# GpSimd's state products in pieces of 256 or 384 columns, retention's decay in VectorE's addition

## The chip, the cores and the metric

The kernel runs on one core of a Trainium2 chip. The metric is the time of the program on the device in microseconds (us). The core has the engines TensorE (PE in the profile; its weight loads are PEld), VectorE (DVE), ScalarE (ACT), GpSimd (POOL) and SyncE (SP, which issues the DMAs). They run side by side and wait for one another by semaphores; each runs its own instructions in the order in which the program gives them.

## The reference

One inference step of a hybrid decoder trunk with two layers, on 16 meta tokens and 256 prompt tokens of one sequence, and on 8 sample sequences of 4 new tokens each: T = 304 columns in all. A layer is

```
proj  = rmsnorm(x) @ w_in
mixed = concat(gated delta net, RG-LRU, GLA, retention) * silu(gate)
x     = x + mixed @ w_out
```

Three of the four mixers carry matrix states. For each sequence and head, after the new tokens,

```
delta      S' = S * exp(g_last)     + sum_j k_j (decay_j v_new_j)^T     128 x 128, 4 heads
GLA        S' = diag(exp(b_last)) S + sum_j k_j (decay_j v_j)^T          64 x 128, 4 heads
retention  S' = S * gamma_h^n       + sum_j k_j (decay_j v_j)^T          64 x 128, 4 heads
```

where n is the number of tokens in the chunk, and b_last and gamma_h are GLA's and retention's decays. Outputs are the normalised x of prompt and samples and all new states, of the prompt and of the eight samples.

## The kernel before

The activations stand transposed, 128 features on the partitions and the 304 tokens in the columns. Each float32 matrix is split into two parts, hi and lo, of TensorE's faster float32 type, and each product takes three matmuls (xh by hi, xl by hi, xh by lo). The weights stream through in units of 128 x 512: a DMA brings `raw`, ScalarE copies it to `hi`, VectorE subtracts to get `lo`. A layer has 48 tiles of the input projection (4 units each) and 16 of the output projection. These products (tiles `main`) are most of TensorE's work.

The mixers run in the gaps of that stream. They are written as Python generators: after a few of the stream's matmuls the builder asks each generator whether its next step may be emitted, by a small model of the engines' clocks (class `Clocks`, prices in `price`, one for each engine and size). The model's prices so set the order in which all engines get their work; on the chip the order is then fixed. One generator runs the four delta heads (two at a time; PSUM tiles named `d`), one GLA's two pairs of heads, one the RG-LRU and retention's two pairs (PSUM tiles `e`).

The states of a head or a pair are one tile `S9` of 128 x 9 x 128: the prompt's state and the eight samples' (tiles `s9.0` to `s9.4` in the rows). Late in `delta_thread` and `pair_thread` each tile goes through the same steps: `reads` multiplies the queries with the old states on TensorE; GpSimd multiplies S9 by the decay; `advance` makes the update on TensorE in PSUM and VectorE adds it to S9. For the samples the update needs the values laid out by sequence: `spread` multiplies the values, repeated n times, by a mask of blocks, into `vm`. Delta calls it once for eight samples, GLA and retention twice for four each.

Three more operations come up below. `lq` is VectorE's subtraction that gives the low part of a squared output for the norm's sum (`totals`: `hq` by ScalarE, `lq` by VectorE, then two matmuls with `onesr`); `zq` is GLA's scaled query for one level of its within-chunk scores, read by a matmul with `zk`; the conv taps are multiply-adds `acc<-ct,par,acc` of the short convolutions. `spots`, four copies on GpSimd for each of two sources, gathers columns into `lxd`, which `reads` takes.

Of the kernel before, what the change touches and what calls it, by code (L numbers as in the profile page):

```python
# [9 lines left out]
F32 = mybir.dt.float32  # L10
# [343 lines left out]
def trunk(ctx: ExitStack, tc: tile.TileContext, I, O):  # L354
    nc = tc.nc
    clk = Clocks()
    pe, act, dve, pool, sp = (Engine(e, k, clk) for e, k in ((nc.tensor, "P"), (nc.scalar, "A"), (nc.vector, "V"),
                                                             (nc.gpsimd, "G"), (nc.sync, "S")))
    mul, add, sub = ALU.mult, ALU.add, ALU.subtract
# [51 lines left out]
    def C(name, a=0, n=1):  # L411
        return cst[:, CC[name] + a:CC[name] + a + n]
# [22 lines left out]
    els = one.tile([128, 12], F32, name="els")  # L435
# [408 lines left out]

    def spread(vm, R, blocks):

        n = blocks.shape[1]
        pool.tensor_mul(vm, R[:, None, 128:256].bitcast(F32).to_broadcast([128, n, 128]),
                        blocks[:, :, None].to_broadcast([128, n, 128]))

    def copies(out, x, n):

# [2 lines left out]
            pool.tensor_copy(out=out[:, 128 * b:128 * b + 16 * n].rearrange("p (u t) -> p u t", u=n),  # L855
                             in_=x[:, None, c:c + 16].to_broadcast([128, n, 16]))

    def advance(tag, S9, p0, n, products):
        ps = pt(tag)
        for i, (out, k, v) in enumerate(products):  # L860
            pe.matmul(ps[out, :128 * n], k, v, start=i == 0 or out.start > 0,
                      stop=i + 1 == len(products) or products[i + 1][0].start > 0)
        dve.tensor_add(S9[:, p0:p0 + n, :], S9[:, p0:p0 + n, :],
                       ps[:, :128 * n].rearrange("p (b v) -> p b v", v=128))

    busy = []

# [31 lines left out]
    def delta_thread(l, p, tag):  # L899
# [4 lines left out]
        K, Q, V, KN, VB, KTL, Eb, AT, qe, egl = ({} for _ in range(10))  # L904
# [16 lines left out]
        for h in range(2):  # L921
            ps = yield from totals(tag, s[h][:, :T])
# [15 lines left out]
        for h in range(2):  # L938
            for src, d, k in ((V, VB, 1), (KN, KTL, 3)):
                d[h] = yield from take(1, src is V)  # L940
                ps = pt(tag)
# [49 lines left out]
        for r in range(2):  # L991
            for u in range(2):
                n = 512 - 16 * u
# [4 lines left out]
        for j in range(15):  # L998
            n, m = 15 - j, j // 2 + 1
# [39 lines left out]
        for h, c, a in hca:  # L1039
            r = slice(32 * a, 32 * a + 32)  # L1040
# [6 lines left out]
        for h, c, a in hca:  # L1047
            r = slice(32 * a, 32 * a + 32)
# [53 lines left out]
        VN, SS, S9 = {}, {}, {}  # L1102
# [7 lines left out]
        ps = pt(tag)  # L1110
# [5 lines left out]
        ps = pt(tag)  # L1116
# [5 lines left out]
        ps = pt(tag)  # L1122
        for h in range(2):
            pe.matmul(ch(ps, h), KN[h][:, 128:256], SS[h][:, 0:128], start=True, stop=True)
        for h in range(2):
            dve.scalar_tensor_tensor(ch(VB[h], 1), ch(ps, h), col[:, 2, 1, hs[h]:hs[h] + 1], ch(VB[h], 1),
                                     op0=mul, op1=add)
        yield
        ps = pt(tag)
# [5 lines left out]
        ps = pt(tag)  # L1135
# [5 lines left out]
        LQ, SL, R = {}, {}, {}  # L1141
# [5 lines left out]
        ps = pt(tag)  # L1147
# [4 lines left out]
        for h in range(2):  # L1152
            R[h], LQ[h] = yield from take(2)
            R[h] = recast(R[h], F32R)
            pk = pt(tag)
            pe.transpose(pk[:, 0:128], KN[h][:, 256:384], ident)
            pool.memset(LQ[h][:, 0:128], 0.0)
            sc = col[:, 3, 2, hs[h]:hs[h] + 1]
            hi_lo(R[h][:, 0:128], pk[:, 0:128], 64, sc)
            activ(LQ[h][0:16, 0:128], pk[0:16, 0:128], AF.Copy, scale=sc[0:16])  # L1160
            spots(lx["d"], 0, slice(0, 128), KN[h])
            spots(lx["d"], 1, slice(0, 128), qe[h])
            give(KN[h])
            yield
            pr = reads(tag, lx["d"], S9[h])
            activ(SL[h][:, 0:128], pr, AF.Copy)
            pool.tensor_mul(S9[h], S9[h], egl[h][:, 2:11, None].to_broadcast([128, 9, 128]))
            yield
        for h in range(2):
            ps = pt(tag)  # L1170
# [6 lines left out]
        for h in range(2):  # L1177
# [4 lines left out]
            ps = pt(tag)  # L1182
# [14 lines left out]
        for h in range(2):  # L1197
            vm = recast((yield from take9()), F32R)
# [84 lines left out]
    def pair_thread(l, p, m, tag):  # L1283
# [23 lines left out]
        S9 = yield from take9()  # L1307
# [44 lines left out]
        if m == "r":  # L1352
            yield from bg.vacant(tag, 2)
            ps2 = [pt(tag), pt(tag)]
            for c, (c0, n) in enumerate(CH):
                for h in range(2):
                    r = slice(64 * h, 64 * h + 64)
# [5 lines left out]
        for h in range(2):  # L1363
            ps = pt(tag)
# [82 lines left out]
        R = yield from take(2)  # L1447
        R = [recast(x, F32R) for x in R]
        ps, ps2 = pt(tag), pt(tag)
# [9 lines left out]
        else:  # L1459
            for h in range(2):  # L1460
                for c in range(2):
                    b = 128 * c + 64 * h
# [4 lines left out]
        for b in range(2):  # L1467
            hm = C("hs", 0, 2)[:, :, None].to_broadcast([128, 2, 64])
            v, k = ps2[:, 128 * b:128 * b + 128], ps2[:, 256 + 128 * b:384 + 128 * b]
# [5 lines left out]
            for h in range(2):  # L1475
                r, own = slice(64 * h + 32, 64 * h + 64), slice(64 * h, 64 * h + 64)
                if sc is None:
                    dve.tensor_sub(R[b][r, own], k[r, own], R[b][r, own].bitcast(F32))
                else:
                    dve.scalar_tensor_tensor(R[b][r, own], k[r, own], sc[r], R[b][r, own].bitcast(F32),  # L1480
                                             op0=mul, op1=sub)
            activ(R[b][:, 128:256], v, AF.Copy)
            dve.scalar_tensor_tensor(R[b][:, 128:256], R[b][:, 128:256].bitcast(F32), C("um", 0), v,
                                     op0=mul, op1=add)
# [7 lines left out]
        ps = pt(tag)  # L1492
        for c in range(2):
            for h in range(2):
                b = 128 * c + 64 * h
# [10 lines left out]
        pr = reads(tag, lx[m], S9)  # L1506
        activ(sel[:, 0:128], pr, AF.Copy)
        if m == "g":
            pool.tensor_mul(S9, S9, els[:, 2:11, None].to_broadcast([128, 9, 128]))
        else:  # L1510
            pool.tensor_scalar(S9[:, 0, :], S9[:, 0, :], C("dec", 3 * p + 1), None, op0=mul)
            pool.tensor_scalar(S9[:, 1:9, :], S9[:, 1:9, :], C("dec", 3 * p + 2), None, op0=mul)
        yield
        sqs_ = yield from take(2)
        yield from bg.vacant(tag, 2)
        ps = [pt(tag), pt(tag)]
        for h in range(2):
            r = slice(64 * h, 64 * h + 64)
# [9 lines left out]
        for h in range(2):  # L1528
# [3 lines left out]
            give(sqs_[h])  # L1532
        give(sel, SS, qe)
        advance(tag, S9, 0, 1, [(slice(64 * h, 64 * h + 64), ktb[:, 64 * h:64 * h + 64], VT[h][0:16, 256:384])
                                for h in range(2)])
        give(*VT)
        vm = recast((yield from take9()), F32R)
        for b in range(2):
            spread(vm[:, 4 * b:4 * b + 4], R[b], C("m4", 0, 4))
        yield  # L1540
        for b in range(2):
            advance(tag, S9, 1 + 4 * b, 4, [(slice(0, 128), R[b][:, 0:128], vm[:, 4 * b:4 * b + 4, :])])
            yield
        give9(recast(vm, F32))
        give(*[recast(x, F32) for x in R])
# [168 lines left out]
    for u, (l, ph, e, q) in enumerate(units):  # L1714
# [30 lines left out]
        a, b = ([t[:, k, :] for k in range(KT)] for t in (xh, xl)) if ph == "in" else (mh, ml)  # L1745
# [21 lines left out]
        if q == NH - 1:  # L1767
# [4 lines left out]
            kind, i = ORDER[e]  # L1772
# [109 lines left out]
```

## Time and profile before

| what | value |
|---|---|
| median of three runs | 1091.02 us (1091.01 to 1096.0) |
| profiled execution, time on the device | 1089.9 us |
| its span, first to last instruction | 1088.0 us |
| TensorE / its weight loads busy | 96% / 91% of the span |
| VectorE / ScalarE / GpSimd busy | 69% / 59% / 38% of the span |
| granted TensorE clock, mean | 0.991 |

The engines' shares are means over the whole span. TensorE is busy nearly throughout, so the waits that count are TensorE's; an idle stretch of another engine costs nothing by itself. Matmuls overlap in the records (one of 304 columns is shown with some 0.30 us and the next starts 0.14 us later), so a wait in the timeline is counted from the end of the last record to the next start.

### The profile page before, as it was taken

What the parts mean: (1) busy time and instruction counts of PE and PEld (TensorE: products, weight loads), DVE (VectorE), ACT (ScalarE), POOL (GpSimd) and SP (SyncE); (2) the same over time, 40 slices, a digit from 0 to 9 for tenths busy, and PEclk for the clock granted to TensorE, in tenths of its full rate; (3) what the DMA queues carried; (4) which work ended last, traced back from release to release, by engine and by line L of the source; (5) the groups of instructions that cost most, each with busy time, mean ns of one, the idle gap of its engine ahead of it and who ended that gap; (6) DMA issues with size and microseconds to landing.
All of it is one profiled execution on the core that took longest, in us unless ns stands there. A gap on an engine that the chain in (4) does not pass through costs nothing.

```text
span 1088.0 us, 23535 instructions
## 1 busy us (share of the span) xinstructions
PE 1042.6 (96%) x8358; PEld 995.1 (91%) x8358; DVE 746.0 (69%) x1457; ACT 639.7 (59%) x1438; POOL 412.9 (38%) x843
## 2 busy tenths in 40 slices
PE   8999999998999999999999998999999999899995
PEld 7899988988998999999999998888999998899995
DVE  5867588798656467556667757878886576765664
ACT  6677954665745766455455876555765466554542
POOL 4423374534518343022222348344254346211110
PEclk9999999999999999999999999999999999999998
DMA  6555434545465555666644545336545663566563
GB/s 212 188 150 187 134 123 138 189 148 190 139 208 186 174 165 181 198 208 211 206 134 144 178 149 164 126 102 212 178 152 159 201 214 122 176 202 207 184 191 138
DMA packets 116893, 186.86 MB, mean 172 GB/s; under 512 B 22184, under 2 KB 45368, under 8 KB 116776
## 3 DMA queue, kind: packets, MB, share of 16 engines
q1 hardware_dynamic: 116776, 185.37, 53.1%
q8 instruction: 65, 1.06, 0.4%
q14 instruction: 52, 0.43, 0.1%
HBM read 164.10 MB, written 19.96 MB: 169 GB/s over the span
## 4 chain that ended last, share of the span: by engine, by line
PE 67%; DVE 13%; DMA 5%; POOL 5%; issue 5%; ACT 4%; SPq 1%; DVEq 0%; ACTq 0%; POOLq 0%
PE main L302 55%; PE e L302 6%; PE d L302 5%; DMA raw<-in_w_in_dram 4%; DVE lo L302 4%; DVE m L302 2%; DVE n L302 2%; POOL m L302 2%; ACT hi L302 1%; DVE zq L302 1%; DVE acc L302 1%; POOL s9.4_4198 L302 1%; POOL n L302 1%; ACT L369 1%; SPq L302 1%
## 5 line engine op out<-in xcount | busy, mean ns | idle before, releaser
L302 PE MATMUL main<-xh,hi 128*128 128x304 f32 (+2 forms) x1488 | 468.7, 315 | 2.8 <-ACT xh L302 2.5
L302 DVE TENSOR_TENSOR lo<-raw,hi 128x512 fp32r<-128x512 f32 (+1 forms) x513 | 391.7, 782 | 101.6 <-ACT hi L302 100.0
L302 PE MATMUL main<-xh,lo 128*128 128x304 f32 (+2 forms) x1488 | 449.8, 302 | 4.2 <-DVE lo L302 4.2
L302 ACT ACTIVATE hi<-raw 128x512 fp32r<-128x512 f32 (+1 forms) x513 | 316.7, 625 | 228.6 <-PE main L302 95.9
L302 PE MATMUL main<-xl,hi 128*128 128x304 f32 (+2 forms) x1488 | 447.6, 301 | 0.4 <-DVE xl L302 0.3
L302 PEld LDWEIGHTS main<-xh,hi 128*128 128x128 f32 x1488 | 281.8, 189 | 14.8 <-issue 6.8
L302 PEld LDWEIGHTS main<-xh,lo 128*128 128x128 f32 x1488 | 281.6, 189 | 7.3 <-DVE lo L302 7.1
L302 PEld LDWEIGHTS main<-xl,hi 128*128 128x128 f32 x1488 | 282.2, 190 | 2.7 <-DVE xl L302 0.9
L302 PE MATMUL main<-m,hi 128*128 128x304 f32 (+1 forms) x1024 | 208.7, 298 | 0.0
L302 PEld LDWEIGHTS main<-m,hi 128*128 128x128 f32 x1024 | 166.5, 188 | 0.0
L302 PE MATMUL main<-m,lo 128*128 128x304 f32 (+1 forms) x512 | 153.3, 299 | 0.0
L302 POOL TENSOR_TENSOR ssq<-ssq,n 128x304 f32<-128x304 f32 (+1 forms) x29 | 34.8, 1200 | 167.4 <-ACT n L302 167.4
L302 PEld LDWEIGHTS main<-m,lo 128*128 128x128 f32 x512 | 96.1, 188 | 0.0
L302 POOL COPY cvo<-ct 128x3 f32<-128x3 f32 x64 | 31.6, 522 | 136.1 <-DVE ct L302 136.0
L302 POOL TENSOR_TENSOR n<-n,n 128x304 f32<-128x304 f32 (+1 forms) x38 | 35.5, 951 | 113.7 <-ACT n L302 69.1
L302 ACT ACTIVATE n<-n 128x304 f32<-128x304 f32 (+4 forms) x118 | 49.5, 438 | 36.0 <-DVE n L302 26.0
L302 DVE TENSOR_TENSOR n<-main,n 128x304 f32<-128x304 f32 (+1 forms) x32 | 14.9, 466 | 61.3 <-PE main L302 51.8
L369 ACT ACT_TABLE_LOAD x35 | 44.9, 1283 | 0.6
L302 DVE SCALAR_TENSOR_TENSOR acc<-ct,par,acc 128x328 f32<-128x328 f32 x64 | 40.7, 636 | 4.9 <-ACT acc L302 3.8
L302 ACT ACTIVATE m<-m 128x304 f32<-128x304 f32 (+5 forms) x95 | 39.3, 431 | 6.9 <-DVE m L302 3.1
L302 DVE TENSOR_TENSOR n<-main,rstd 128x304 f32<-128x304 f32 (+1 forms) x42 | 19.5, 465 | 26.4 <-PE main L302 26.0
L302 ACT ACTIVATE n<-e 128x304 f32<-128x304 f32 (+5 forms) x67 | 19.6, 307 | 28.9 <-PE e L302 15.4
(416 smaller groups left out, 1334.5 us busy)
## 6 DMA issues: line engine op xcount, KB each, us to landing
raw<-in_w_in_dram SPq DMA_DIRECT2D x383, 256.0 KB
raw<-in_w_out_dram SPq DMA_DIRECT2D x128, 256.0 KB
n<-o_dram SPq DMA_DIRECT2D x28, 152.0 KB
o_dram<-m SPq DMA_DIRECT2D x19, 152.0 KB
m<-in_x_dram SPq DMA_DIRECT2D x16, 152.0 KB
n<-in_x_dram SPq DMA_DIRECT2D x16, 152.0 KB
xs_dram<-n SPq DMA_DIRECT2D x16, 152.0 KB
n<-xs_dram SPq DMA_DIRECT2D x16, 152.0 KB
```

Of the source, the lines that this page charges most:

```text
L302: r = f(*a, **k)
L369: nc.scalar.preload_act_table_set(want[0])
```

## The change

GpSimd's decay of a state tile, one product of 9 x 128 = 1152 columns, becomes three products of 3 x 128 = 384 (function `decay`), for delta and GLA. `spread` makes one product for each two samples, 256 columns, where it made one of 1024 (delta) or 512 (GLA, retention). Retention's decay, two single-input scalings on GpSimd, is left out; `advance` gets the decay as an argument and VectorE's addition becomes a multiply-add, S9 * decay + update. The values computed are the same.

```diff
@@ -844,9 +844,14 @@
 
     def spread(vm, R, blocks):
 
-        n = blocks.shape[1]
-        pool.tensor_mul(vm, R[:, None, 128:256].bitcast(F32).to_broadcast([128, n, 128]),
-                        blocks[:, :, None].to_broadcast([128, n, 128]))
+        for i in range(0, blocks.shape[1], 2):
+            pool.tensor_mul(vm[:, i:i + 2], R[:, None, 128:256].bitcast(F32).to_broadcast([128, 2, 128]),
+                            blocks[:, i:i + 2, None].to_broadcast([128, 2, 128]))
+
+    def decay(S9, by):
+
+        for i in range(0, 9, 3):
+            pool.tensor_mul(S9[:, i:i + 3], S9[:, i:i + 3], by[:, i:i + 3, None].to_broadcast([128, 3, 128]))
 
     def copies(out, x, n):
 
@@ -855,13 +860,16 @@
             pool.tensor_copy(out=out[:, 128 * b:128 * b + 16 * n].rearrange("p (u t) -> p u t", u=n),
                              in_=x[:, None, c:c + 16].to_broadcast([128, n, 16]))
 
-    def advance(tag, S9, p0, n, products):
+    def advance(tag, S9, p0, n, products, by=None):
         ps = pt(tag)
         for i, (out, k, v) in enumerate(products):
             pe.matmul(ps[out, :128 * n], k, v, start=i == 0 or out.start > 0,
                       stop=i + 1 == len(products) or products[i + 1][0].start > 0)
-        dve.tensor_add(S9[:, p0:p0 + n, :], S9[:, p0:p0 + n, :],
-                       ps[:, :128 * n].rearrange("p (b v) -> p b v", v=128))
+        o, x = S9[:, p0:p0 + n, :], ps[:, :128 * n].rearrange("p (b v) -> p b v", v=128)
+        if by is None:
+            dve.tensor_add(o, o, x)
+        else:
+            dve.scalar_tensor_tensor(o, o, by, x, op0=mul, op1=add)
 
     busy = []
 
@@ -1164,7 +1172,7 @@
             yield
             pr = reads(tag, lx["d"], S9[h])
             activ(SL[h][:, 0:128], pr, AF.Copy)
-            pool.tensor_mul(S9[h], S9[h], egl[h][:, 2:11, None].to_broadcast([128, 9, 128]))
+            decay(S9[h], egl[h][:, 2:11])
             yield
         for h in range(2):
             ps = pt(tag)
@@ -1506,10 +1514,7 @@
         pr = reads(tag, lx[m], S9)
         activ(sel[:, 0:128], pr, AF.Copy)
         if m == "g":
-            pool.tensor_mul(S9, S9, els[:, 2:11, None].to_broadcast([128, 9, 128]))
-        else:
-            pool.tensor_scalar(S9[:, 0, :], S9[:, 0, :], C("dec", 3 * p + 1), None, op0=mul)
-            pool.tensor_scalar(S9[:, 1:9, :], S9[:, 1:9, :], C("dec", 3 * p + 2), None, op0=mul)
+            decay(S9, els[:, 2:11])
         yield
         sqs_ = yield from take(2)
         yield from bg.vacant(tag, 2)
@@ -1532,14 +1537,15 @@
             give(sqs_[h])
         give(sel, SS, qe)
         advance(tag, S9, 0, 1, [(slice(64 * h, 64 * h + 64), ktb[:, 64 * h:64 * h + 64], VT[h][0:16, 256:384])
-                                for h in range(2)])
+                                for h in range(2)], C("dec", 3 * p + 1) if m == "r" else None)
         give(*VT)
         vm = recast((yield from take9()), F32R)
         for b in range(2):
             spread(vm[:, 4 * b:4 * b + 4], R[b], C("m4", 0, 4))
         yield
         for b in range(2):
-            advance(tag, S9, 1 + 4 * b, 4, [(slice(0, 128), R[b][:, 0:128], vm[:, 4 * b:4 * b + 4, :])])
+            advance(tag, S9, 1 + 4 * b, 4, [(slice(0, 128), R[b][:, 0:128], vm[:, 4 * b:4 * b + 4, :])],
+                    C("dec", 3 * p + 2) if m == "r" else None)
             yield
         give9(recast(vm, F32))
         give(*[recast(x, F32) for x in R])
```

The planner prices the new instructions and the order of all engines moves with them from the first cut product on. Three places:

VectorE, layer 1, second delta pair, the second head's norm (its `lq` is the last one of a delta head), rows of before:

```order
L302 TENSOR_TENSOR lo<-raw,hi 128x512 x2
L302 TENSOR_TENSOR m_12588<-n_154,m_12587 128x288
L302 TENSOR_TENSOR m_12590<-n_5487,m_12589 128x288
L302 TENSOR_TENSOR lo<-raw,hi 128x512
L302 TENSOR_TENSOR lq<-g_144,hq 128x304
L302 TENSOR_TENSOR n_4200<-main,rstd 128x288
L302 TENSOR_TENSOR lo<-raw,hi 128x512
```

and of the change:

```order
L302 TENSOR_TENSOR s9.1_10369<-s9.1_10369,d 128x128
L302 TENSOR_TENSOR lo<-raw,hi 128x512 x2
L302 TENSOR_TENSOR lq<-n_167,hq 128x304
L302 TENSOR_TENSOR n_12715<-main,rstd 128x288
L302 TENSOR_TENSOR lo<-raw,hi 128x512 x2
L302 SCALAR_TENSOR_TENSOR g_147<-g_147,par,n_167 128x304
```

Ahead of this head's `lq` stood two subtractions of the gated output (`m`) and a `lo`; now `lo` twice alone.

GpSimd, layer 1, second delta pair, from the first head's decay (`egl`) on to the second head's gathering copies (`lxd`); rows of before:

```order
L302 TENSOR_TENSOR s9.1_11583<-s9.1_11583,egl 128x1152
L302 MEMSET g_144 128x128
L302 COPY lxd<-g_138 128x16
L302 COPY lxd<-g_138 128x3x4 x2
L302 COPY lxd<-g_138 128x2x4
L302 COPY lxd<-m_7452 128x16
L302 COPY lxd<-m_7452 128x3x4 x2
L302 COPY lxd<-m_7452 128x2x4
L302 TENSOR_TENSOR s9.0_4398<-s9.0_4398,egl 128x1152
```

and of the change:

```order
L302 TENSOR_TENSOR s9.0_11594<-s9.0_11594,egl 128x384 x3
L302 TENSOR_TENSOR s9.3_12530<-n_12204,cst 128x256 x2
L302 TENSOR_TENSOR s9.3_12530<-n_12205,cst 128x256 x2
L302 TENSOR_TENSOR n_157<-n_157,n_5929 128x288
L302 TENSOR_TENSOR g_140<-g_140,n_5378 128x288
L302 MEMSET n_167 128x128
L302 COPY lxd<-g_146 128x16
L302 COPY lxd<-g_146 128x3x4 x2
```

The second head's copies stood right behind the first head's decay; now the pieces of a retention pair's spread (`s9.3`), two gating products and a memset stand between.

GpSimd, layer 1, the spread of the last GLA pair and what is next to it; rows of before:

```order
L302 TENSOR_TENSOR g_146<-g_146,n_5970 128x304
L302 MEMSET g_146 128x16
L302 TENSOR_SCALAR s9.0_4398<-s9.0_4398,cst 128x128
L302 TENSOR_SCALAR s9.0_4398<-s9.0_4398,cst 128x1024
L302 TENSOR_TENSOR s9.2_11289<-n_10787,cst 128x512
L302 TENSOR_TENSOR s9.2_11289<-m_10788,cst 128x512
L302 TENSOR_TENSOR s9.3_171<-s9.3_171 80x15 x2
```

and of the change:

```order
L302 TENSOR_TENSOR g_134<-g_134,m_7481 128x304
L302 MEMSET g_134 128x16
L302 TENSOR_TENSOR s9.2_11411<-m_10886,cst 128x256 x2
L302 TENSOR_TENSOR s9.2_11411<-m_10887,cst 128x256 x2
L302 TENSOR_TENSOR s9.0_11535<-n_11148,cst 128x256 x2
L302 TENSOR_TENSOR s9.0_11535<-n_11149,cst 128x256 x2
L302 TENSOR_TENSOR s9.3_171<-s9.3_171 80x15 x2
```

Retention's two scalings are gone, and the spread of the first retention pair (`s9.0_11535`), which stood 14 rows further on, follows that of the last GLA pair: eight pieces in a row.

## Rows read from the trace of the kernel before

**Rows 1.** The page: busy time of each engine, share of the span, instructions.
```profile
PE 1042.6 (96%) x8358; PEld 995.1 (91%) x8358; DVE 746.0 (69%) x1457; ACT 639.7 (59%) x1438; POOL 412.9 (38%) x843
```

**Rows 2.** Windows view, three stretches: length, busy time (instructions), clock, DMA.
```profile
183.00:420.00 237.00, 229.05 (x1955) 215.25 (x1949) 164.03 (x332) 145.40 (x353) 112.60 (x229) 1.00 0.52 169
420.00:667.00 247.00, 246.04 (x1787) 240.98 (x1786) 159.22 (x284) 146.43 (x299) 71.92 (x133) 1.00 0.57 182
667.00:960.00 293.00, 278.71 (x2445) 262.23 (x2446) 214.75 (x446) 168.96 (x411) 132.30 (x273) 0.99 0.52 167
```

**Rows 3.** Timeline of TensorE: start, duration, instruction, [wait <- what ended it].
```profile
247.08 0.42 PE L302 MATMUL e<-zq,zk 128*64 128x64 f32 x7 [2.74 <-DVE zq L302]
...
419.58 0.41 PE L302 MATMUL d<-lq,onesr 128*128 128x304 f32 x1 [1.44 <-DVE lq L302]
...
733.25 0.41 PE L302 MATMUL e<-lq,onesr 128*128 128x304 f32 x1 [1.71 <-DVE lq L302]
...
746.61 0.50 PE L302 MATMUL d<-s9.1_10128,m 128*128 128x512 f32 x1 [2.18 <-DVE s9.2_3655 L302]
...
909.59 0.66 PE L302 MATMUL d<-s9.0_4398,lxd 128*32 128x128 f32 x11 [0.80 <-POOL lxd L302]
...
922.76 0.41 PE L302 MATMUL e<-lq,onesr 128*128 128x304 f32 x1 [0.54 <-DVE lq L302]
...
939.32 0.62 PE L302 MATMUL d<-lq,onesr 128*128 128x304 f32 x1 [3.03 <-DVE lq L302]
```

**Rows 4.** Timeline of GpSimd: three long products.
```profile
416.84 2.35 POOL L302 TENSOR_TENSOR s9.4_5925<-n,cst 128x1024 fp32r<-128x1024 f32 x1
419.15 2.13 POOL L302 TENSOR_TENSOR s9.1_5958<-n,cst 128x1024 fp32r<-128x1024 f32 x1
...
741.00 2.40 POOL L302 TENSOR_TENSOR s9.1_10128<-m,cst 128x1024 fp32r<-128x1024 f32 x1 [1.45 <-PE d L302]
```

**Rows 5.** Timeline of VectorE: two-input operations beside products, and alone.
```profile
165.63 0.63 DVE L302 TENSOR_TENSOR zq<-n,m 64x152 f32<-64x152 f32 x2
...
244.71 2.23 DVE L302 TENSOR_TENSOR zq<-m,m 64x152 f32<-64x152 f32 x2
...
417.36 2.16 DVE L302 TENSOR_TENSOR lq<-n,hq 128x304 fp32r<-128x304 f32 x1
419.44 2.38 DVE L302 TENSOR_TENSOR lo<-raw,hi 128x512 fp32r<-128x512 f32 x1
...
741.57 3.25 DVE L302 SCALAR_TENSOR_TENSOR acc<-ct,par,acc 128x328 f32<-128x328 f32 x2
...
934.06 4.22 DVE L302 TENSOR_TENSOR m<-n,m 128x288 fp32r<-128x288 f32 x2
938.20 0.68 DVE L302 TENSOR_TENSOR lo<-raw,hi 128x512 fp32r<-128x512 f32 x1
938.80 0.46 DVE L302 TENSOR_TENSOR lq<-g,hq 128x304 fp32r<-128x304 f32 x1
```

**Rows 6.** Groups of GpSimd's instructions by shape: count | busy, mean ns | idle before.
```profile
L302 POOL TENSOR_TENSOR s9.1_5407<-n,cst 128x512 fp32r<-128x512 f32 x2 | 2.0, 1046 | 0.0
...
L302 POOL TENSOR_TENSOR s9.2_3562<-n,cst 128x1024 fp32r<-128x1024 f32 x1 | 1.9, 1890 | 0.0
...
L302 POOL TENSOR_TENSOR s9.0_4398<-s9.0_4398,els 128x1152 f32<-128x1152 f32 x1 | 2.1, 2110 | 0.0
```

**Rows 7.** Timelines of GpSimd and VectorE: retention's scalings, and lo beside one.
```profile
284.60 3.67 POOL L302 TENSOR_SCALAR s9.2_3655<-s9.2_3655,cst 128x128 f32<-128x128 f32 x2
...
898.84 3.95 POOL L302 TENSOR_SCALAR s9.4_10071<-s9.4_10071,cst 128x128 f32<-128x128 f32 x2 [7.58 <-PE e L302]
...
286.60 1.29 DVE L302 TENSOR_TENSOR lo<-raw,hi 128x512 fp32r<-128x512 f32 x2
```

**Rows 8.** Timeline of VectorE: additions and a multiply-add with a PSUM operand.
```profile
286.40 0.28 DVE L302 TENSOR_TENSOR s9.3_171<-s9.3_171,e 128x128 f32<-128x128 f32 x1
...
740.37 0.67 DVE L302 TENSOR_TENSOR s9.0_4398<-s9.0_4398,e 128x512 f32<-128x512 f32 x1
...
898.36 0.35 DVE L302 SCALAR_TENSOR_TENSOR s9.1_11583<-n,egl,d 128x128 f32<-128x128 f32 x1 [0.20 <-PE d L302]
```

## The prediction

> **What bounds the kernel now.** I read the busy line of the page first: TensorE is busy in 1042.6 of 1088.0 us, VectorE in 746.0, GpSimd in 412.9 [rows 1]. The matrix products are the same before and after, so time can be won or lost only in TensorE's idle 45 us. Next I ask where that idle time lies and which of it the change can reach. The first long product that is cut stands at 183 us (GLA's decay in layer 0); up to there the order of both programs is the same, and the mixers run in two stretches only. The windows view gives TensorE 237.00 - 229.05 = 7.95 us of idle time from 183 to 420 us, 1.0 us from 420 to 667 us (layer 0's output projection and the start of layer 1), and 293.00 - 278.71 = 14.29 us from 667 to 960 us [rows 2]. From 960 us on the last output projection runs with no state work left. So 22.2 us are within reach.
>
> Then I went through TensorE's waits in these stretches and looked at what GpSimd did while the operation that was waited for stood in its queue. Seven waits lie beside one of the long products, together 12.4 us [rows 3]; the reader is to see that six of them name VectorE (zq, lq, s9) and not GpSimd. The link is in the timelines. At 416.84 us a 1024-column product starts on GpSimd; VectorE's lq, which takes 0.46 us by itself, begins at 417.36 and lasts 2.16 us, until just after the product's end at 419.19 [rows 4, 5]. The lo behind it then meets the second product (419.15 to 421.28) and lasts 2.38 us. So a VectorE operation with two operands in SBUF does not run while a GpSimd product with two inputs runs; it waits to the product's end. At 741.57 two conv taps take 3.25 us in this way, at 934.06 two subtractions take 4.22 us, at 244.71 a pair of zq takes 2.23 us against 0.63 us for such a pair elsewhere [rows 5]. The remaining 9.8 us of the 22.2 have other causes.
>
> **The change, part by part.** (1) *Price of a piece.* Undisturbed, a product of 512 columns takes 1.046 us, of 1024 columns 1.890, of 1152 columns 2.110 [rows 6]. That is 0.20 us and 1.65 ns a column; so a piece of 256 columns takes 0.62 us and one of 384 columns 0.83 us (estimates from these rows). There are 12 decays (three pieces instead of one: +0.40 us each), 8 delta spreads (four instead of one: +0.61) and 16 half spreads of GLA and retention (two instead of one: +0.20): 36 instructions become 100, and 57.2 us of GpSimd time become 70.0 us, 12.8 more. GpSimd is idle for 675 us, so this costs nothing by itself; what it costs where its cover is gone is in the rivals.
>
> (2) *Retention's decay.* Two single-input scalings leave GpSimd in each of four pairs; they take 3.67 to 3.95 us there [rows 7], so 15.2 us, and GpSimd ends about 2.5 us lighter. Twelve additions on VectorE become multiply-adds. With 128 columns and a PSUM operand an addition takes 0.28 us and a multiply-add 0.35 [rows 8]. The trace has no multiply-add of 512 columns from PSUM; between no surcharge beyond 0.67 us for the addition [rows 8] and one that grows with the columns (0.28) I take the measured 0.07: 12 x 0.07 = 0.8 us, at most 2.5. It lies on an engine that is free for 342 us, behind state products on which no TensorE wait of this trace hangs: 0 on the path.
>
> Do the scalings that leave also free VectorE? The row says no: beside the one from 284.60 to 288.27 two lo ran in 1.29 us, 0.65 each [rows 7]. The Trainium skill ("SBUF — State Buffer", on the shared port pair) states that a VectorE operation with two SBUF inputs is shut out by a GpSimd operation that reads SBUF, whichever starts first holding it to its end; this scaling reads SBUF, so by that rule lo would have waited, and the trace disagrees. If TensorE's waits per us of product (12.4 / 57.2 = 0.22) held for 15.2 us of scalings too, the rule would take 3.3 us more off; by the row it is 0, and I use 0.
>
> (3) *What the shorter pieces give at the seven places.* When a product is cut, VectorE's waiting operation goes in after at most one piece (0.62 or 0.83 us), but GpSimd's next piece goes in behind it: lo at 419.44 had to let the second product by, though it was itself in line. So the first operation of VectorE's queue gains much, the third little. Place by place, with the order where I looked at it:
> - 939.32, wait 3.03: lq stands behind two subtractions and a lo, beside two products in a row. In the new order lq stands behind lo alone, and two 288-column products separate the two sets of pieces. About 0.5 remains: -2.5.
> - 419.58, 1.44: lq is first in line; its 1.7 us of delay becomes at most 0.62. -1.1.
> - 746.61, 2.18: four taps in a row; each can meet a piece, so in the same order nothing is won, if the taps go elsewhere all of it. Half: -1.1.
> - 909.59, 0.80: the second head's gathering copies queue behind the first head's decay on GpSimd. In the new order the first head's spread and other products stand between the two heads, and its pieces end long before the copies: -0.8.
> - 733.25, 1.71, and 922.76, 0.54: halves of 512 columns already; lq is second or third in line. Half: -1.1 together.
> - 247.08, 2.74: two zq in line, delayed by 1.6 us together; two pieces still cost up to 1.2. -0.6.
>
> Sum: -7.2 us; the bounds are 0 and -12.4. (4) *The rest of the order.* The planner prices the pieces on GpSimd and lays the small work between the weight products anew from 183 us on. The other 9.8 us of waits are drawn again; I take 0 with 4 us to either side (the size of the two or three largest of them). The sum is made on the profiled execution: 1089.9 us, of which 1088.0 are span. 1089.9 - 7.2 = 1082.7; the median of the runs lies 1.1 above that execution, so I predict 1084.
>
> **Rivals.** *The pieces hold VectorE as much as the whole did.* For it: GpSimd's piece goes in again after each VectorE operation, and at 733.25 and 922.76 halves did not prevent a wait. Then only places where lq is first in line gain, some 2.5 us: 1088.5; or TensorE's share of 0.22 per us of product stays, and 70.0 us give 15.2 instead of 12.4: 1093.8. Against it: the two largest losses (3.03 and 1.44) come from whole products of 1024 columns, and halves lost 0.54 and 1.71 in sixteen, the whole ones 9.4 in eight. Chance 0.30, between these two times.
>
> *Everything at the seven places goes.* Then 1091.0 - 12.4 = 1078.6. For it: in the new order the spreads at three of them stand away from lq and the taps. Against it: lq still follows a lo within a piece's reach. Chance 0.15.
>
> *Slower: the new order stacks pieces.* GpSimd gets the eight 256-column pieces of layer 1's last GLA pair and first retention pair in a row, 8 x 0.62 = 5.0 us in which every two-input operation of VectorE pays a piece, with a norm's lq among them; four of its queue's operations would wait 2.5 us, and a wait of TensorE for lq or lo follows. Once three places of this kind cost 4 us each and nothing else is won, the time is 1091.0 - 7.2 + 12.6 = 1096.4; it decides from 12.7 us of such new waits on, more than all waits of this kind now. Chance 0.09.
>
> **How the numbers follow.** The forecast (about 1081 to 1087, 7.2 us give or take 3) has 0.46. I take 0.5% (5.5 us) as what a measurement of this kernel can tell. Faster than 1085.6: all of the 0.15, and 0.38 of the 0.46, so 0.53. Within 0.5%: 0.08 of the forecast and the 0.30 of the first rival, 0.38. Slower: 0.09. The range goes from 1078 (all seven places gone, a little to spare) to 1092, which takes in most of the first rival and leaves out the slower one: about 2 in 10 outside.
>
> **What would show it.** Right: no VectorE operation with two SBUF inputs lasts over about 1.6 us any more beside a GpSimd product; a 256-column piece takes 0.62 us and a 384-column one 0.83 when undisturbed; no single-input scaling is left on GpSimd; retention's additions are 0.07 us longer; TensorE's idle time from 183 to 960 us falls from 23.2 to about 16 us, and lq, zq and s9 lose most in the list of its waits. Wrong: these waits stay although the long operations are gone (then the pieces hold VectorE in turn), or they vanish and others of the same size stand elsewhere (then it is the new order), above all at the eight pieces in a row.

## The result, and the profile after

The changed kernel takes **1086.35 us** (median; 1083.02 to 1092.48) where the kernel before takes 1091.02 in the same session, 4.7 us less. The ratio goes by the means, 1086.35 against 1092.54 us: 0.9943 [0.9924, 0.9963], 0.57% faster. The forecast was 1084, range 1078 to 1092. The first profiled execution happened to be the slowest of its runs (1092.48 us); the rows below are of a second one, 1085.45 us with a span of 1083.2, which stands nearer to the median. TensorE's idle time from 183 to 960 us agrees in both (19.2 us in the one and 19.0 in the other); the waits for n at 345 us and for hi are shorter in the first, 1.21 and 1.50 us.

Busy line of the page, changed kernel:
```profile
PE 1043.3 (96%) x8358; PEld 995.4 (92%) x8358; DVE 736.6 (68%) x1457; ACT 635.2 (59%) x1434; POOL 418.0 (39%) x899
```
The same 8358 matrix products [rows 1]; GpSimd has 56 instructions more (64 more products, 8 scalings less), and VectorE is 9.4 us less busy although its work is the same or a little more: its busy time holds the time in which an operation stands and waits for a GpSimd product.

Windows of the changed kernel (columns as in [rows 2]):
```profile
183.00:420.00 237.00, 231.11 (x1960) 218.06 (x1955) 169.53 (x339) 144.49 (x353) 118.69 (x257) 0.99 0.54 171
420.00:667.00 247.00, 246.14 (x1790) 241.22 (x1790) 156.05 (x277) 143.32 (x295) 72.24 (x137) 1.00 0.58 181
667.00:960.00 293.00, 280.70 (x2468) 263.24 (x2467) 206.92 (x450) 171.59 (x416) 129.81 (x299) 0.99 0.53 168
```
TensorE's idle time is 5.89 + 0.86 + 12.30 = 19.0 us, where it was 23.2 [rows 2]: 4.2 us less, most of the 4.8 us by which this span is shorter than that of before.

TensorE's waits from 183 us on in the changed kernel, by what ended them (us in total, times, longest):
```profile
PE e L302 <- DVE zq L302: 3.9, 5, 1.8
PE e L302 <- POOL n L302: 2.7, 2, 2.2
PE main L302 <- ACT hi L302: 2.0, 1, 2.0
PE e L302 <- DVE s9.4_10192 L302: 1.8, 1, 1.8
...
PE d L302 <- DVE lq L302: 0.6, 2, 0.4
```
lq, which ended waits of 3.03 and 1.44 us before [rows 3], is down to 0.4 at most. In its place stand hi, a state (s9.4) and, in the timeline below, a spread on GpSimd (s9.1), which [rows 3] do not have. The timeline of TensorE shows the largest:
```profile
246.98 0.52 PE L302 MATMUL e<-zq,zk 128*64 128x64 f32 x10 [1.82 <-DVE zq L302]
...
753.36 0.50 PE L302 MATMUL d<-s9.1_10296,n 128*128 128x512 f32 x1 [1.29 <-POOL s9.1_10296 L302]
...
800.16 0.44 PE L302 MATMUL e<-s9.4_10192,lxg 128*32 128x128 f32 x5 [1.78 <-DVE s9.4_10192 L302]
...
856.41 0.40 PE L302 MATMUL main<-xh,hi 128*128 128x288 f32 x1 [2.05 <-ACT hi L302]
...
910.93 0.44 PE L302 MATMUL d<-s9.0_11594,lxd 128*32 128x128 f32 x5 [0.81 <-POOL lxd L302]
```
Prices, from the groups by shape (columns as in [rows 6]):
```profile
L302 POOL TENSOR_TENSOR s9.2_11411<-m,cst 128x256 fp32r<-128x256 f32 x4 | 2.3, 613 | 0.0
...
L302 POOL TENSOR_TENSOR s9.3_171<-s9.3_171,els 128x384 f32<-128x384 f32 x3 | 2.4, 827 | 5.4 <-PE e L302 5.4
...
L302 DVE SCALAR_TENSOR_TENSOR s9.2_3687<-s9.2_3687,cst,e 128x512 f32<-128x512 f32 x2 | 1.5, 748 | 0.1
...
L302 POOL TENSOR_TENSOR s9.1_5860<-n,cst 128x256 fp32r<-128x256 f32 x4 | 3.7, 949 | 0.0
```
Undisturbed, a piece takes 0.61 and 0.83 us, as worked out from [rows 6]; retention's addition of 512 columns takes 0.75 instead of 0.67 us [rows 8]. The last row shows what the estimate did not have: beside VectorE work a 256-column piece lasts 0.95 us, because the waiting goes both ways.

### The profile page after: what moved, and what is told of

Same layout as the page of the kernel before. It is cut to its first block, busy times and chain, and to the rows that moved or that the text cites. A ratio compares the mean times of both kernels' runs of the same rounds, so it can differ in the third digit from the quotient of the medians.

```text
span 1090.4 us, 23569 instructions
## 1 busy us (share of the span) xinstructions
PE 1047.6 (96%) x8358; PEld 999.7 (92%) x8358; DVE 738.9 (68%) x1457; ACT 634.8 (58%) x1434; POOL 414.8 (38%) x899
## 3 DMA queue, kind: packets, MB, share of 16 engines
q8 instruction: 65, 1.06, 0.4%
## 4 chain that ended last, share of the span: by engine, by line
PE 66%; DVE 12%; POOL 7%; DMA 6%; ACT 4%; issue 4%; SPq 1%; DVEq 0%; ACTq 0%; POOLq 0%
PE main L302 54%; PE d L302 6%; PE e L302 6%; DMA raw<-in_w_in_dram 3%; DVE lo L302 3%; DVE n L302 3%; DVE m L302 2%; POOL m L302 2%; DVE zq L302 1%; ACT n L302 1%; SPq L302 1%; POOL s9.1_5930 L302 1%; POOL s9.4_4196 L302 1%; ACT L369 1%; POOL n L302 1%
## 5 line engine op out<-in xcount | busy, mean ns | idle before, releaser
L302 DVE TENSOR_TENSOR lo<-raw,hi 128x512 fp32r<-128x512 f32 (+1 forms) x513 | 395.7, 790 | 99.6 <-ACT hi L302 97.8
L302 DVE TENSOR_TENSOR n<-main,rstd 128x304 f32<-128x304 f32 (+1 forms) x41 | 18.9, 461 | 21.1 <-PE main L302 19.3
```

The costliest lines, as they stand in the source:

```text
L302: r = f(*a, **k)
```

## The experiments

All were timed in five rounds beside the kernel before. In the kernels named old_order the order of every engine is that of before: the planner is charged one whole product, and GpSimd's instruction is cut behind its back. That separates the size of the pieces from the order that the planner makes of them.

**The pieces alone, in the old order (old_order_pieces).**
```
 def spread(vm, R, blocks):
     n = blocks.shape[1]
-    pool.tensor_mul(vm, <R over n blocks>, <blocks>)
+    for i in range(0, n, 2):
+        nc.gpsimd.tensor_mul(vm[:, i:i + 2], <R over 2 blocks>, <blocks i, i + 1>)
+    clk.op("G", price("G", "tensor_mul", size(vm), vm, 0), [vm], [R, blocks])
```
and the decays likewise, three blocks at a time; retention's scalings stay.

> The order of before on every engine, with each long two-input product of GpSimd cut into the pieces of the change (the planner is still charged for one whole product; retention's scalings stay on GpSimd). If the shorter pieces alone give the gain, because VectorE's waiting operation gets in after one piece: 1091.0 - 4.7 = about 1086.5, ratio 0.994 to 0.997, and the waits of TensorE for lq at 420, 734, 923 and 939 us shrink. Rival, the gain is the new order: 1090 to 1092, ratio 0.999 to 1.002. Rival, the pieces hold VectorE in turn for 12.8 us more of GpSimd's time: 1093 to 1094, ratio 1.002 to 1.003.

Measured: 1084.27 us, 0.9935 [0.9915, 0.9956]. The pieces alone give the gain. At 418 and 934 us, GpSimd, VectorE and TensorE (timelines, to be held against [rows 3 to 5]):
```profile
417.13 3.70 POOL L849 TENSOR_TENSOR s9.4_5951<-n,cst 128x256 fp32r<-128x256 f32 x4
...
417.65 0.88 DVE L302 TENSOR_TENSOR lq<-n,hq 128x304 fp32r<-128x304 f32 x1
...
934.09 1.65 DVE L302 TENSOR_TENSOR m<-n,m 128x288 fp32r<-128x288 f32 x2
935.67 1.10 DVE L302 TENSOR_TENSOR lo<-raw,hi 128x512 fp32r<-128x512 f32 x1
936.69 0.88 DVE L302 TENSOR_TENSOR lq<-g,hq 128x304 fp32r<-128x304 f32 x1
...
937.62 0.41 PE L302 MATMUL d<-lq,onesr 128*128 128x304 f32 x1 [1.29 <-DVE lq L302]
```
lq takes 0.88 us, 0.42 more than its own 0.46 [rows 5]; so does lo (1.10 against 0.68). TensorE's idle time from 183 to 960 us is 18.9 us, as in the changed kernel. At these two places every two-input operation of VectorE lets one piece by, and every piece lets one operation by. That is not so everywhere. In the same execution one lo lets four pieces in a row by:
```profile
843.09 2.33 POOL L849 TENSOR_TENSOR s9.1_11556<-n,cst 128x256 fp32r<-128x256 f32 x4
...
843.10 2.88 DVE L302 TENSOR_TENSOR lo<-raw,hi 128x512 fp32r<-128x512 f32 x1
```
The pieces take about their undisturbed time, and lo takes 2.2 us more than its 0.68. No wait of TensorE hangs on it. No run tells what makes the one case or the other.

**Pieces and retention, in the old order (old_order_both).** The kernel above, and retention's scalings replaced by the multiply-add:
```
-            pool.tensor_scalar(S9[:, 0, :], ...)
-            pool.tensor_scalar(S9[:, 1:9, :], ...)
...
+            nc.vector.scalar_tensor_tensor(o, o, by, x, op0=mul, op1=add)
```

> The order of before with the whole change in it: pieces, and retention's decay in VectorE's addition (the planner is charged as before, so nothing else moves). Retention's part costs nothing and frees nothing on TensorE's path: the same time as the pieces alone in the old order, within 1.5 us. If its single-input scalings did hold VectorE, it would be about 3.3 us faster than that kernel. Against before: 0.994 to 0.997 if the pieces carry the gain, 0.999 to 1.002 if the new order does.

Measured: 1084.12 us, 0.9943 [0.9921, 0.9966]; against the pieces alone no difference. The retention part is worth nothing that can be measured.

**The new order with whole products (new_order_whole).** The changed kernel, but the planner is charged the pieces while GpSimd gets one instruction:
```
-            pool.tensor_mul(vm[:, i:i + 2], ...)
+        nc.gpsimd.tensor_mul(vm, <R over n blocks>, <blocks>)
+        for i in range(0, n, 2):
+            clk.op("G", price("G", "tensor_mul", 256, vm, 0), [vm[:, i:i + 2]], [R, blocks])
```

> The order of the change on every engine, with each decay and spread made as one whole product again (the planner is still charged for the pieces; retention's decay stays in VectorE's addition). If the pieces carry the gain: back to 1090 to 1092, ratio to before 0.999 to 1.001, with long waits for lq, zq or s9 at the products. If the new order carries it: 1085 to 1087.5, ratio 0.994 to 0.997.

Measured: 1088.68 us (one of twelve executions took 3500.29), 0.9972 [0.9954, 0.9991]: the order by itself gives 2.1 us (its kernel before: 1090.78). Its waits from 183 us on:
```profile
PE e L302 <- DVE zq L302: 5.2, 6, 2.7
...
PE d L302 <- DVE lq L302: 2.4, 4, 0.9
...
PE e L302 <- DVE s9.4_10149 L302: 1.8, 1, 1.8
PE main L302 <- ACT hi L302: 1.5, 2, 1.2
```
lq is down to 0.9 at most without a single piece, since the order has taken it away from the spreads; zq keeps its 2.7. And the waits for s9.4 and hi are here too, so they come with the order and not from the pieces.

**The changed kernel once more (after_again).**

> The changed kernel once more, beside the others and for a second profile, since the first one's 1092.5 us lies above all its other executions (1083.0 to 1090.4). Expected 1086.3 us, ratio 0.992 to 0.997. If the 3 us that the first profile loses before 183 us, where both programs have the same order, are of that execution alone, they are not in this profile.

Measured: 1086.92 us, 0.9959 [0.9938, 0.998]. The intervals of this and of the old order with pieces overlap; that the old order is 2 us better is likely from the medians but not settled.

**One two-input product more behind each spread (dose_two).** The kernel before, with 24 extra products of 512 columns on a tile that nothing else reads:
```
+        nc.gpsimd.tensor_mul(<dose as 4x128>, <dose as 4x128>, <C("m4", 0, 4) broadcast>)
```

> The kernel before with one more GpSimd instruction behind each of its 24 spreads: a two-input product of 512 columns on a tile that nothing else uses (about 1.05 us each, 25 us of GpSimd in all; the order of all else as before, the planner isn't charged). If a two-input product of GpSimd keeps VectorE's two-operand operations out, TensorE's waits grow by the share that they had: 25 x 0.22 = 5.5 us, 1093 to 1099, ratio 1.002 to 1.008. Rival, only the lateness of GpSimd's own later work counts: the same time as with the one-input instruction.

Measured: 1099.62 us, 1.0073 [1.0045, 1.0102]. GpSimd, VectorE and TensorE at 941 us:
```profile
941.18 1.25 POOL L851 TENSOR_TENSOR dose<-dose,cst 128x512 f32<-128x512 f32 x1
942.40 2.10 POOL L302 TENSOR_TENSOR s9.3_12916<-g,cst 128x1024 fp32r<-128x1024 f32 x1
944.47 1.49 POOL L851 TENSOR_TENSOR dose<-dose,cst 128x512 f32<-128x512 f32 x1
...
942.67 2.38 DVE L302 TENSOR_TENSOR lo<-raw,hi 128x512 fp32r<-128x512 f32 x1
944.97 1.31 DVE L302 TENSOR_TENSOR lq<-g,hq 128x304 fp32r<-128x304 f32 x1
...
946.34 0.62 PE L302 MATMUL d<-lq,onesr 128*128 128x304 f32 x1 [4.71 <-DVE lq L302]
```
lq now pays for a 512-column product as well (1.31 against 0.46), and TensorE's wait there grows from 3.03 [rows 3] to 4.71.

**The same with one input (dose_one).**
```
+        nc.gpsimd.tensor_scalar(dose[:, 0:320], dose[:, 0:320], C("m4", 0), None, op0=mul)
```

> The same as the kernel with the added two-input products, but each added instruction is a one-input scaling of 320 columns (about as long, 1.05 us by retention's rows). If only two-input products keep VectorE out: no VectorE operation is stretched by it and the time is that of before plus what GpSimd's lateness costs, ratio 0.998 to 1.002. By the Trainium skill (SBUF — State Buffer, the shared port pair: any GpSimd operation that reads SBUF shuts out a VectorE operation with two SBUF inputs) it would cost as much as the two-input one, 1.002 to 1.008.

Measured: 1091.04 us, 0.9994 [0.9975, 1.0013]: nothing, although the 24 scalings keep GpSimd longer (median 1.52 us) than the 24 products of dose_two (1.27). At 938 us, GpSimd and VectorE:
```profile
938.44 1.57 POOL L851 TENSOR_SCALAR dose<-dose,cst 128x320 f32<-128x320 f32 x1
939.98 2.16 POOL L302 TENSOR_TENSOR s9.3_12916<-g,cst 128x1024 fp32r<-128x1024 f32 x1
...
939.06 0.93 DVE L302 TENSOR_TENSOR lo<-raw,hi 128x512 fp32r<-128x512 f32 x1
939.91 0.46 DVE L302 TENSOR_TENSOR lq<-g,hq 128x304 fp32r<-128x304 f32 x1
```
lo runs inside the scaling, 0.25 us longer than its 0.68, and lq comes at its bare 0.46 us, ahead of the second product; the scaling takes 1.57 us where undisturbed ones take 1.08. The two slow each other a little, but lo does not wait for the scaling's end (940.01 us); TensorE's wait there even falls to 1.58 us, because the scaling stands between two products and lets the line of VectorE through.

**Which of the products (old_order_spreads, old_order_decays).** old_order_pieces without the decays' pieces, and without the spreads':
```
-            decay(S9[h], egl[h][:, 2:11])                    # old_order_spreads
+            pool.tensor_mul(S9[h], S9[h], egl[h][:, 2:11, None].to_broadcast([128, 9, 128]))
...
-        for i in range(0, n, 2):                             # old_order_decays
-            nc.gpsimd.tensor_mul(vm[:, i:i + 2], ...)
+        pool.tensor_mul(vm, <R over n blocks>, <blocks>)
```

> The order of before with only the spreads in pieces of 256 columns; the 12 decays stay whole. Six of the seven waits stand beside spreads: by that the gain is nearly that of all pieces, 1084 to 1086, ratio 0.9935 to 0.996. Rival, the decays matter as much (they are over 40% of the products' time): about half, 1087 to 1088.5, ratio 0.9965 to 0.998.

> The order of before with only the 12 decays in pieces of 384 columns, the spreads whole. The spreads alone gave 0.9927 and all pieces 0.9935, so the decays give nothing: 1090 to 1092.5, ratio 0.999 to 1.002. Rival, either part alone takes away the same waits: about 1086, ratio 0.995 to 0.997.

Measured: spreads 1084.62 us, 0.9927 [0.9901, 0.9952]; decays 1090.47 us, 0.9999 [0.9978, 1.0021]. The spreads carry everything; with the decays alone the waits of [rows 3] at the spreads stay as they were (2.18 and 3.03 us are found unchanged). That the decays' pieces add nothing to the spreads' is as far as these intervals tell: 0.9927 and 0.9935 for all pieces are not told apart.

**How short (old_order_512, old_order_384, old_order_delta256, old_order_128).** All in the old order. The first three cut delta's eight spreads only (2 x 512; 384 + 384 + 256; 4 x 256), the last cuts every long product into single blocks of 128:
```
-        for i in range(0, n, 2):
+        for i in range(0, n, 4):        # 512; for 384 and 256: 3 and 2 where n == 8, else 4; for 128: 1
```

> The order of before; only delta's eight spreads are cut, each into two products of 512 columns (GLA's and retention's half spreads have 512 already, the decays stay whole). If the longest single wait counts, this takes part of the gain: 1086 to 1088.5, ratio 0.996 to 0.998, between whole (1) and 256 columns (0.9927). Rival: with fewer pieces in line it is as good as 256 columns, 0.992 to 0.995.

> The order of before; delta's eight spreads in three pieces each (384, 384 and 256 columns), all else whole. By the reading that GpSimd runs one piece between any two operations of VectorE that stand in line, as long as pieces are left, each of the four operations up to lq at 939 us waits about 0.63 us (0.42 at 256 columns, 0.84 at 512): the wait of TensorE there is 3.0 - (3.4 - 2.5) = about 2.1 us, between 1.3 and 3.0; lq at 420 us waits about 0.63. Time 1086.5 to 1089, ratio 0.996 to 0.9985. Rival, some length between 256 and 512 decides at once: the time of 512 (1090.5) or of 256 columns (1084.5).

> The order of before; only delta's eight spreads are cut, into 256 columns; GLA's and retention's half spreads stay at 512 columns and the decays whole. Delta's spreads carry the waits at 247, 420, 747 and 939 us (9.4 of the 12.4): most of the gain of all spreads, 1084.5 to 1086.5, ratio 0.9935 to 0.997; the waits at 734 (1.7) and 923 us (0.5) stay. Rival, the half spreads carry as much: 1087 to 1088.5.

> The order of before with every long product in pieces of 128 columns (8 or 9 of them instead of 4 or 3; about 0.41 us each, so GpSimd has 12 x 1.6 + 24 spreads' 0.8 to 1.7, some 43 us more than whole). If what counts is how long VectorE's operation waits for one piece: as good as or better than 256 and 384 columns, 1082.5 to 1085, ratio 0.992 to 0.995. Rival, the total time of the products counts too, as each operation in line pays a piece: worse, 1086 to 1089, ratio 0.996 to 0.999; GpSimd's own copies and products come late and TensorE waits for POOL.

Measured: 512: 1090.45 us (one of twelve executions took 4244.8), 0.9995 [0.9971, 1.0019]; 384: 1086.96, 0.9969 [0.9949, 0.9988]; 256: 1085.55, 0.9948 [0.9923, 0.9973]; 128 (all products): 1088.91, 0.9984 [0.9961, 1.0008]. Halving the two spreads at 934 us buys nothing. VectorE and TensorE with 512 columns:
```profile
935.16 2.51 DVE L302 TENSOR_TENSOR m<-n,m 128x288 fp32r<-128x288 f32 x2
937.60 1.52 DVE L302 TENSOR_TENSOR lo<-raw,hi 128x512 fp32r<-128x512 f32 x1
939.04 1.30 DVE L302 TENSOR_TENSOR lq<-g,hq 128x304 fp32r<-128x304 f32 x1
...
940.40 0.62 PE L302 MATMUL d<-lq,onesr 128*128 128x304 f32 x1 [3.00 <-DVE lq L302]
```
With 384:
```profile
931.01 2.08 DVE L302 TENSOR_TENSOR m<-n,m 128x288 fp32r<-128x288 f32 x2
933.01 1.09 DVE L302 TENSOR_TENSOR lo<-raw,hi 128x512 fp32r<-128x512 f32 x1
934.03 1.09 DVE L302 TENSOR_TENSOR lq<-g,hq 128x304 fp32r<-128x304 f32 x1
...
935.17 0.41 PE L302 MATMUL d<-lq,onesr 128*128 128x304 f32 x1 [1.94 <-DVE lq L302]
```
Here is the count that decides. Four operations of VectorE stand in line up to lq (m, m, lo, lq). Two whole products meet the two m, at (4.22 - 2 x 0.41) / 2 = 1.7 us each, and lo and lq then run free: 3.4 us. Four halves meet all four operations at 1.30 - 0.46 = 0.84 us: 3.4 us again, and TensorE waits 3.00 instead of 3.03. With 384 columns each m and lq lose 0.63 and lo loses 0.41, since it meets the rest of 256 columns: 2.3, and the wait is 1.94; with 256 it is 4 x 0.42 = 1.7 and the wait is 1.29. Each step in the sum (1.1, 0.6) is the step of the wait (1.06, 0.65) to 0.1 us. (The 0.41 for one m alone is half of the pair's time in rows where no product stands beside it, 0.81 us in the changed kernel at 930.00.)

And the other end, 128 columns, GpSimd and TensorE:
```profile
736.11 4.84 POOL L849 TENSOR_TENSOR s9.1_10199<-m,cst 128x128 fp32r<-128x128 f32 x8
...
741.01 0.50 PE L302 MATMUL d<-s9.1_10199,m 128*128 128x512 f32 x1 [1.82 <-POOL s9.1_10199 L849]
```
The spread as a whole takes 4.84 us where it took 2.40 [rows 4], and now TensorE waits for GpSimd itself.

## Why the prediction was right, step by step

The seven places, from the timelines of TensorE (us of wait; in brackets what is another than in [rows 3]):

| place, before | before | pieces, old order | whole, new order | the change | forecast for the change |
|---|---|---|---|---|---|
| 247 zq | 2.74 | 1.83 | 2.74 | 1.82 | 2.14 |
| 420 lq | 1.44 | 0.15 | 0.89 | 0.42 (spread) | 0.34 |
| 733 lq, 923 lq | 2.25 | 0.99 | 0.47 (a delta head's lq) | 0.23 (a delta head's lq) | 1.15 |
| 747 s9 | 2.18 | 0.92 (lo) | 1.17 (spread) | 1.53 (spread, twice) | 1.08 |
| 910 lxd | 0.80 | 0.66 | 0.76 (first head) | 0.81 (first head) | 0 |
| 939 lq | 3.03 | 1.29 | 0.63 | 0 | 0.53 |
| sum | 12.4 | 5.8 | 6.7 | 4.8 | 5.2 |

- **Step (3), the sum.** 12.4 - 4.8 = 7.6 us were saved where 7.2 were forecast. That the totals agree so well is partly luck: the rows miss by -0.9 to +0.8 us, and their errors cancel. The mechanism (a two-input product of GpSimd keeps a two-input operation of VectorE out) is shown by dose_two against dose_one. The row for 939 was credited to the new order, rightly: whole products in the new order leave 0.63. But the pieces alone would have taken 1.74 off as well; order and pieces each remove much of the same waits, so 6.6 for the one and 5.7 for the other do not add up.
- **The term of 0.8 at 910 us** held for the wait that it was about, and a new wait of that size stands one head earlier. In the kernel before the first head's reads (`s9.1_11583`) wait for nothing and the second head's (`s9.0_4398`) wait 0.80 [rows 3]; in the changed kernel the second head's (`s9.1_10369`) wait for nothing, as foreseen, and the first head's (`s9.0_11594`) wait 0.81. TensorE of the kernel before, then TensorE and GpSimd of the changed one:
```profile
905.34 0.86 PE L302 MATMUL d<-s9.1_11583,lxd 128*32 128x128 f32 x18
...
921.49 0.86 PE L302 MATMUL d<-s9.1_10369,lxd 128*32 128x128 f32 x18
...
909.77 0.20 POOL L302 MEMSET n<- 128x128 f32 x1 [20.32 <-DVE n L302]
```
  Ahead of the first head's copies GpSimd was idle for 20.32 us, until VectorE let it go on. Taking a blocker out of a queue pays only up to the next thing that is late, which the prediction did not look for. With whole products in the new order the same wait stands there (0.76), so it comes with the order.
- **At 747 us** the taps no longer end the wait, and it passed to the spread itself: 1.17 us with whole products in the new order, 1.53 with pieces, which take longer than a whole product (3.61 us at 749.70, against 2.40 [rows 4]).
- **Step (1)** held: 0.61 and 0.83 us undisturbed. Pieces beside VectorE work are longer (0.95 us), which the sum did not have: GpSimd was to end 2.5 us lighter and is 5.1 us busier (418.0 against 412.9 [rows 1]). TensorE waits for a spread only in the rows of 420 and 747 and with 128 columns.
- **Step (2)** held. The forecast took 0 by the row of a scaling with lo beside it [rows 7], against the rule in the Trainium skill ("SBUF — State Buffer", on the shared port pair), by which any GpSimd operation that reads SBUF shuts such an operation out. The measurement decides for the row: 24 scalings cost nothing (0.9994), 24 products 0.73%. But that row was not the only one. Beside the scalings from 356.79 to 360.51 us the kernel before has two subtractions of which the second takes 1.30 us, where such a one takes 0.46 alone:
```profile
357.36 1.75 DVE L302 TENSOR_TENSOR m<-n,m 128x304 fp32r<-128x304 f32 x2 [1.24 <-ACT m L302]
```
  The lo behind it runs freely inside the same scaling (0.68 us). So a one-input scaling can hold a two-input operation for a while; it does not hold it to its end, and here that cost no time that can be measured.
- **The idea behind the halves** ("the first operation of VectorE's queue gains much, the third little") was right in direction and is sharper now: at 939 us the delay of the critical operation is the smaller of the number of pieces and of the operations in line, times the wait for one piece. It is no rule for every place: the lo at 843.10 us is one operation and paid for four pieces, against the prediction's "at most one piece". The prediction used 0.62 us for that wait; it is 0.42.
- **Step (4)** was taken as 0 with 4 us to either side, and the idle time from 183 to 960 us was to fall to about 16 us. It fell to 19.0: of the 7.6 us saved at the seven places 3.4 came back elsewhere (7.6 - 4.2), which is more than the 2.4 us that separate 1086.4 from 1084. They stand before hi (2.05; ScalarE had been idle for 6.68 us until a weight transfer landed), s9.4 (1.78) and n at 345 us (2.24, where the kernel before has 1.14 and 0.51, and the first profile of the changed kernel 1.21). Worked out in the same way, 12.4 - 5.8 = 6.6 us saved against 23.2 - 18.9 = 4.3 of idle time, 2.3 came back in the old order with pieces, and 12.4 - 6.7 = 5.7 against 23.2 - 22.5 = 0.7, 5.0, in the new order with whole products. In the old order the next zq, at 250.55 us, waits 1.44 where it waited 0.60. So part of it returns in any order, and the waits for hi and s9.4 belong to the new one; the waits of the new order were not taken apart one by one.
- **The rivals.** That pieces hold VectorE as much as the whole is what happens with 512 columns, and not with 256. The stack of eight pieces left no wait of TensorE for lq above 0.4 us. The slower rival's sum does not come out: three places of 4 us are 12, not 12.6, and if nothing else is won, 7.2 may not be taken off.
- **The signs.** No two-input operation was to last over 1.6 us beside a GpSimd product. In the changed kernel two lo still take 2.13 and 2.33 us (329.73, 333.33), each beside two products of 304 columns that the change does not cut.

So the version to keep is a smaller one: the old order with the spreads cut to 256 columns, 1084.62 us, 0.9927, without the decays' pieces, the retention edit or a new plan.

## What to carry to other kernels

Before cutting a long two-input product of GpSimd, count the two-input operations of VectorE that stand in line up to the one that TensorE needs: at 939 us pieces helped only once there were more of them than operations in line, and with 128 columns they hurt, since their sum made GpSimd's result the late one. Work of GpSimd with one input stood beside VectorE, even between two products, at no cost that could be measured. Where a planner re-lays the program for a local edit, charge it the old price once, so that the edit and the new order are measured apart.

## What the runs showed of the hardware that was not expected

TensorE's clock took part, and the prediction has no term for it. Some of the long waits are followed, or overlapped, by a stretch at half the clock. Windows of the kernel before around the two largest waits after 700 us (the clock is the third number from the end):
```profile
747.70:751.10 3.40, 3.13 (x13) 3.04 (x13) 3.40 (x8) 1.23 (x5) 0.89 (x1) 0.50 0.61 191
938.80:942.20 3.40, 2.88 (x12) 2.88 (x13) 1.97 (x6) 1.58 (x3) 0.00 (x0) 0.51 0.23 80
```
and of the changed kernel:
```profile
248.50:251.90 3.40, 3.30 (x21) 2.86 (x20) 3.23 (x12) 0.58 (x1) 2.55 (x11) 0.51 0.36 119
801.50:804.90 3.40, 3.40 (x21) 2.95 (x21) 1.88 (x4) 1.94 (x6) 3.32 (x6) 0.50 0.50 154
```
That is 1.2 GHz where the rest runs at 2.4, so each of these stretches costs up to 1.7 us (half of 3.40) beyond the wait itself. In this execution of the changed kernel the two of before are gone with their waits, and two others stand behind the waits for zq (1.82) and s9.4 (1.78): no gain in sum between these two executions. In the profiled execution of old_order_both the stages have the full clock, 1.00 where the changed kernel shows 0.99 (first and third stage):
```profile
183.00:420.00 237.00, 231.04 (x1978) 217.65 (x1977) 165.08 (x336) 146.46 (x356) 111.76 (x254) 1.00 0.53 170
...
667.00:960.00 293.00, 282.24 (x2491) 265.61 (x2486) 211.39 (x453) 173.28 (x419) 132.54 (x300) 1.00 0.54 170
```
and its span, 1080.3 us, is the shortest of all that were profiled. Its wait of 1.82 us for zq at 245.70 is the same as that of the changed kernel, and no half-clock stretch follows. So the length of the wait does not decide it; what does was not settled.

Over all executions the clock differs. Its mean is 0.9885 for the kernel before in the session of the first four experiments, 0.9914 for the changed kernel and also for the pieces in the old order, and 0.9909 for whole products in the new order. An estimate: 0.003 of 1088 us is 3 us, a good part of what each of the three gains, and in the last more than its idle time gained (0.7 us). The gain does not need it: with only delta's spreads cut to 256 columns the clock is 0.9891, that of before in the same session 0.9895, and the ratio 0.9948. How much of the changed kernel's gain is clock and how much is idle time stays open; the 2 us between the old order and the new do not show in the clock, whose mean is the same in both.
